# Fourier stage: the first group's folds moved into the last RG-LRU head, DFT tables from buffers of their own, last sums in other PSUM banks

## The chip, the cores and the metric

The kernel runs on one core of one Trainium2 chip. A core has five engines with instruction queues of their own: TensorE (PE in the profile), VectorE (DVE), ScalarE (ACT), GpSimd (POOL) and SyncE (SP); SP is used here only to issue DMA transfers. The metric is the time of one execution on the device in microseconds (us), as the median of several runs.

## The reference, cut to what matters

The reference is a trunk of two layers over 1024 latent tokens with a prefix of 256 context tokens, width 1024. The first layer projects its normed input with one matrix and splits the result in two halves with a SiLU gate each: an RG-LRU (eight heads of 128 channels, a recurrence run in both directions) and a Fourier mixer (four groups of 256 channels); both halves, gated, go through one output projection. The second layer is a retention layer, which this change leaves alone. The Fourier mixer is a 2D DFT over tokens and channels of each group, of which the real part is kept, and then one small matrix for each group:

```python
def fourier_branch(z, w_f):
    B_, T, W = z.shape
    zg = z.astype(jnp.float32).reshape(B_, T, FNET_GROUPS, FNET_GROUP_DIM)
    f = jnp.real(jnp.fft.fft2(zg, axes=(1, 3), norm='ortho'))
    y = jnp.einsum('btgi,gij->btgj', f, w_f.astype(jnp.float32))
    return y.reshape(B_, T, W).astype(z.dtype)

def even_mixer(h, hc, w_in, w_out, ...):
    ...
    ya, yca = rglru_branch(xa, xca, conv_w, conv_b, wa, ba, wx, bx, lam)
    yb = fourier_branch(xb, w_f)
    y = jnp.concatenate([ya * jax.nn.silu(ga), yb * jax.nn.silu(gb)], axis=-1) @ w_out
```

## The kernel before, in words

**Split operands.** Every product that must keep float32 accuracy is made from two parts: `split` casts an operand to fp32r (the high part, on ScalarE, or on VectorE with `he="v"`) and subtracts to get the low part (on VectorE, or on GpSimd with `le="g"`). `acc3` then issues three matmuls: high by high, high by low, low by high. A weight tile therefore passes through a DMA, a cast and a subtraction before TensorE can use it.

**The RG-LRU heads** (the loop over `n`, lines 437 to 482). Each head projects its input, makes gates, and ends in three scans on VectorE, an addition and a product with the gate `sga`, whose result goes to `ya_d` in DRAM. While head 7 runs, the projection of the first two channel tiles of the Fourier stage is already made (`four_z(8)` and `four_z(9)`).

**The Fourier groups** (the loop over `g`, lines 544 to 678). For each of the two channel tiles of a group, the tokens are *folded*: the first half of the sequence plus and minus the mirrored second half (`ze`, and `zc` for the context), with two single columns scaled apart (`zsp`). The folds of the two tiles are combined (`zss`, and `ze` and `zc` in place) and split (`zxh`, `zxl`, `zh`, `zl`). TensorE multiplies them with the combined channel matrix (`pa`, `pac`, `pn`), ScalarE and VectorE split the sums (`ah`, `al`), and the second set of products (`pd`, function `dftmm`, and `pcx` for the context) uses the DFT tables `dh` and `dl`. The result `y` is put together on VectorE, multiplied with the gate `sgb` (line 677) and written to `yb_d` by a DMA on SP's queue (line 678). Each group has two such halves, `ct` 0 and 1. The tables are made once, in group 0, by `dft_tables`: four raw pieces `dr` are loaded into the buffers of the ring `wr`, which the projection weights use too, cast on VectorE, and subtracted on GpSimd.

**PSUM.** Tiles with the tag `aux` share four banks, tiles with the tag `mm` four others. `pa`, `pn`, `pd`, `pcx` and the columns of the modulation vectors (`mod_a`, `mod_c`) are `aux`; the projections `pj` and `po` are `mm`.

**The output projection** begins when the Fourier stage ends. Its weights come through `w1tile`: a load into `wr` (printed as `wr<-in_wout`) by SP, a cast on ScalarE, a low part on VectorE or GpSimd in turn. Their buffers lie in pools that are allocated after the Fourier pools `four_in`, `four_out` and `fconst` are released, so in memory that these held.

**What sets the order.** The program is written for a scheduler that orders the instructions of each engine from dependencies and priorities; `tc.high_priority(offset=...)` moves what is written under it ahead by that offset. Each engine, and SP's DMA queue, then works strictly in that order: an instruction that waits holds back all that stand behind it in its queue. A pool's place in memory comes from the order in which pools are allocated, and a tile that lies over released memory waits for the last users of what lay there. `mod_next` makes one column block of the modulation vectors: `mod_a` on TensorE from a loaded `modw`, a copy `modr` on VectorE, and in a later call `mod_c` on TensorE, which VectorE reads for `sh` and `gs`.

Of the kernel before, what the change touches and what calls it, by code (L numbers as in the profile page):

```python
# [8 lines left out]
F32 = mybir.dt.float32  # L9
# [7 lines left out]
P = 128  # L17
# [8 lines left out]

OW0, OW1, OWE, OWF = [120, 140, 120, 150]
# [28 lines left out]
def _build(ctx, nc, tc, I, out, dbg):  # L56
# [306 lines left out]
    fz = pool("four_z")  # L363
    def channel_mats(g):
        cd = wp.tile([P, 2, 2, P], F32, tag="wr", name="cd", bufs=WRB)
        nc.sync.dma_start(cd, I["cd"])
        fw = fz.tile([P, 2, 256], F32, tag="fw", name="fw")
        nc.sync.dma_start(fw, I["fw"][g])
        pc = ps.tile([P, 2, 256], F32, tag="aux", name="cwp", bufs=4)
        for m in range(2):  # L370
            for k in range(2):
                mm(pc[:, m, :], cd[:, k, m, :], fw[:, k, :], k == 0, k == 1)
        f_ = fz.tile([P, 2, 256], F32, tag="cwf", name="cwf")
        h_ = fz.tile([P, 2, 256], F32R, tag="cwh", name="cwh")
        l_ = fz.tile([P, 2, 256], F32R, tag="cwl", name="cwl")
        nc.scalar.copy(f_, pc)
        split(f_, h_, l_)
        return f_, h_, l_
# [59 lines left out]
    for n in range(8):  # L438
# [4 lines left out]
        if n < 7:  # L443
            xa, gw = lru_in(n + 1)
        else:
            cw0 = channel_mats(0)
            zf0 = four_z(8)
# [24 lines left out]
        nga = gate_a(n + 1) if n < 7 else four_z(9)  # L472
# [10 lines left out]
    zs0 = [zf0, nga]  # L483
# [32 lines left out]

    fc = pool("fconst")
    cts = fc.tile([P, 260], F32, name="cts")
    nc.scalar.dma_start(cts, I["dftx"])
    dh = fc.tile([P, 2, 1028], F32R, name="dh")  # L520
    dl = fc.tile([P, 2, 1028], F32R, name="dl")
    COSE, COSO, SINE, SINO = (0, 258), (258, 256), (514, 256), (770, 258)
    fp = pool("four_out")
    fq = pool("four_in")
# [10 lines left out]
    def dft_tables():  # L535
        for j in range(2):
            for b in range(2):
                s = slice(b * 514, (b + 1) * 514)
                dr = wp.tile([P, 514], F32, tag="wr", name="dr", bufs=WRB)
                nc.sync.dma_start(dr, I["dftc"][:, j, s])  # L540
                split(dr, dh[:, j, s], dl[:, j, s], he="v", le="g")

    for g in range(4):
# [3 lines left out]
        zz = []  # L547
        for ct in range(2):
            z = zs0[ct]
            if g:  # L550
                z = four_z(8 + 2 * g + ct)
                mod_next()
            s2 = fq.tile([P, 2], F32, tag=f"zsp{ct}", name="zsp", bufs=1)
            nc.vector.tensor_scalar(out=s2[:, 0:1], in0=z[:, 512:513], scalar1=1.0 / 32, scalar2=None, op0=ALU.mult)
            nc.vector.tensor_scalar(out=s2[:, 1:2], in0=z[:, T + 129:T + 130], scalar1=1.0 / 16, scalar2=None, op0=ALU.mult)
            t = [s2]
            for e, op in ((0, ALU.add), (1, ALU.subtract)):
                w = fq.tile([P, 512], F32, tag=f"ze{e}{ct}", name=f"ze{e}", bufs=1)
                wc = fq.tile([P, P], F32, tag=f"zc{e}{ct}", name=f"zc{e}", bufs=1)
                (nc.vector if ct else nc.gpsimd).tensor_tensor(out=w.rearrange("p (two n) -> p n two", two=2),  # L560
                                        in0=z[:, 0:512].rearrange("p (n two) -> p n two", two=2),
                                        in1=z[:, T:512:-1].rearrange("p (n two) -> p n two", two=2), op=op)
                nc.vector.tensor_tensor(out=wc, in0=z[:, T + 1:T + 129], in1=z[:, NT + 1:T + 129:-1], op=op)
                t += [w, wc]
            zz.append(t)
        zx = [fq.tile([1, 512], F32R, tag=f"zx{p}", name=f"zx{p}") for p in "hl"]
        split(zz[0][1][0:1, :], *zx)
        zcx, zsx = zz[0][2][0:1, :], zz[0][0][0:1, :]
        for i, (a, b) in enumerate(zip(*zz)):
            if i == 0:  # L570
                zs = fq.tile([P, 2], F32, tag="zss", name="zss")
                nc.vector.tensor_tensor(out=zs, in0=a, in1=b, op=ALU.add)
            else:
                nc.vector.tensor_tensor(out=b, in0=a, in1=b, op=ALU.add if i < 3 else ALU.subtract)
                if i > 2:
                    nc.gpsimd.memset(b[0:1, :], 0.0)
        zf = []
        for e in range(2):
            zh = fq.tile([P, 512], F32R, tag=f"zh{e}", name=f"zh{e}")
            zl = fq.tile([P, 512], F32R, tag=f"zl{e}", name=f"zl{e}")  # L580
            split(zz[1][1 + 2 * e], zh, zl)
            zf.append((zz[1][2 + 2 * e], zh, zl))
        sgb = [gate_b(2 * g), None]
        if not g:
            dft_tables()
# [34 lines left out]
        for ct in range(2):  # L620
# [13 lines left out]
            def dftmm(e, par, blk):  # L634
                next(side, None)
                o = ps.tile([P, 512], F32, tag="aux", name="pd", bufs=4)
                b0, bn = blk
                ah, al = A[e, par]
                for j in range(2):
                    acc3(o[:, :bn], ah[:, j, cs], al[:, j, cs], dh[:, j, b0:b0 + bn], dl[:, j, b0:b0 + bn], j == 0, j == 1)  # L640
# [42 lines left out]
    fq.release()  # L683
    fp.release()
    fc.release()
    fz.release()
# [733 lines left out]
```

## Time and profile before

| | before |
|---|---|
| median of 3 runs | 1973.33 us |
| lowest and highest run | 1972.36 and 1985.31 us |
| the profiled run's own time | 1979.08 us |
| span of its trace | 1977.3 us |
| TensorE busy, share of the span | 95% |
| VectorE, ScalarE, GpSimd busy | 68%, 44%, 31% |
| mean granted TensorE clock | 0.97 |

The rows of the profile come from one execution, the profiled run; its time is 5.75 us above the median. TensorE is the busiest engine. Times in the timelines are in us from the start of the span. What an engine waited for stands in brackets in a timeline, as the idle time ahead of an instruction and the instruction that ended it.

### The profile page before, as it was taken

How to read it: one execution, taken by the hardware profiler on the slowest of the kernel's cores; microseconds unless marked ns; L12 is line 12 of the kernel's file. 1: busy time of each engine (PE TensorE's matmuls, PEld its weight loads, DVE VectorE, ACT ScalarE, POOL GpSimd, SP SyncE). 2: the span in 40 equal slices, each digit the busy share in tenths (PEclk: the TensorE clock that was granted, in tenths of full speed). 3: DMA queues.
4: the chain of work that ended last, by engine and by line, in shares of the span. 5: the costliest groups of instructions: out<-in, count | busy, mean ns of one | idle time of the engine just before them, and what ended most of it. 6: DMA issues, size and time to landing. Idle time of an engine off the chain costs nothing. (4 is left out here: it accounts for less than half of the span.)

```text
span 1977.3 us, 27858 instructions
## 1 busy us (share of the span) xinstructions
PE 1878.3 (95%) x10418; PEld 1592.5 (81%) x10418; DVE 1342.3 (68%) x1952; ACT 877.7 (44%) x1459; POOL 621.5 (31%) x407
## 2 busy tenths in 40 slices
PE   7999999899999999998988999999999799999997
PEld 3788888788888788887877889898898577877886
DVE  6787788742334515687798877778776685767766
ACT  5576667522222433364632433424334455554552
POOL 2411211302112241243455242252430133444444
PEclk8999999979999899999999999999999899999998
DMA  7221222322212362345834746547457656565544
GB/s 281 90 78 62 96 67 89 107 82 97 90 58 72 129 210 94 127 154 156 275 95 146 244 127 213 183 146 256 125 179 255 221 194 194 179 200 175 184 126 155
DMA packets 167559, 297.18 MB, mean 150 GB/s; under 512 B 15200, under 2 KB 94464, under 8 KB 166272
## 3 DMA queue, kind: packets, MB, share of 16 engines
q1 hardware_dynamic: 135824, 273.20, 42.5%
q10 hardware_dynamic: 31504, 22.16, 3.5%
q8 instruction: 82, 1.34, 0.3%
q14 instruction: 53, 0.43, 0.1%
q0 software_dynamic: 96, 0.04, 0.0%
HBM read 212.51 MB, written 82.84 MB: 149 GB/s over the span
## 5 line engine op out<-in xcount | busy, mean ns | idle before, releaser
L63 POOL TENSOR_TENSOR wl<-wr,wh 128x512 fp32r<-128x512 f32 (+1 forms) x80 | 149.4, 1870 | 376.3 <-ACT wh L69 365.9
L69 ACT CAST w<-wr 128x1024 fp32r<-128x1024 f32 x140 | 146.7, 1049 | 195.9 <-PE pst L58 115.7
L65 DVE TENSOR_TENSOR w<-wr,w 128x1024 fp32r<-128x1024 f32 x112 | 145.1, 1295 | 112.1 <-ACT w L69 112.1
L58 PE MATMUL pj<-xh,wl 128*128 128x512 f32 x512 | 203.0, 396 | 3.3 <-POOL wl L63 3.3
L58 PE MATMUL pj<-xh,wh 128*128 128x512 f32 x512 | 204.6, 401 | 1.0 <-ACT wh L69 0.6
L58 PE MATMUL pj<-xl,wh 128*128 128x512 f32 x512 | 202.7, 396 | 1.2 <-POOL xl L63 1.1
L58 PE MATMUL pst<-xh,w 128*128 128x512 f32 x512 | 164.8, 396 | 6.4 <-DVE w L65 6.4
L58 PE MATMUL po<-xh,w 128*128 128x512 f32 x512 | 163.9, 393 | 0.0
L63 POOL TENSOR_TENSOR w<-wr,w 128x1024 fp32r<-128x1024 f32 x28 | 70.8, 2530 | 165.6 <-ACT w L69 164.0
L58 PEld LDWEIGHTS pst<-xh,w 128*128 128x128 f32 x512 | 97.3, 190 | 27.0 <-DVE w L65 6.9
L58 PEld LDWEIGHTS pj<-xh,wl 128*128 128x128 f32 x512 | 97.0, 189 | 24.5 <-POOL wl L63 4.1
L58 PEld LDWEIGHTS pj<-xh,wh 128*128 128x128 f32 x512 | 96.7, 189 | 23.3 <-issue 1.4
L58 PEld LDWEIGHTS pj<-xl,wh 128*128 128x128 f32 x512 | 96.8, 189 | 22.1 <-POOL xl L63 2.1
L58 PEld LDWEIGHTS po<-xh,w 128*128 128x128 f32 x512 | 96.2, 188 | 19.7 <-issue 0.5
L69 ACT CAST st<-st 128x256 fp32r<-128x256 f32 (+2 forms) x128 | 53.6, 433 | 124.0 <-DVE st L969 56.2
L69 ACT CAST wh<-wr 128x512 fp32r<-128x512 f32 (+1 forms) x80 | 63.3, 793 | 92.3 <-DMA wr<-in_win 33.4
L58 PE MATMUL pds<-vp,kh 128*128 128x512 f32 x288 | 93.6, 407 | 8.7 <-ACT kh L1118 8.4
L58 PE MATMUL pst<-xl,w 128*128 128x512 f32 x256 | 100.6, 393 | 0.0
L58 PE MATMUL po<-stp,qt 128*128 128x512 f32 x384 | 97.8, 401 | 2.8 <-DVE stp L65 2.4
L58 PE MATMUL po<-xl,w 128*128 128x512 f32 x256 | 99.9, 390 | 0.0
L58 PE MATMUL pst<-w,xh 128*128 128x256 f32 x512 | 93.0, 284 | 0.7 <-DVE w L65 0.7
L58 PE MATMUL pj<-xc,wh 128*128 128x256 f32 x512 | 91.2, 278 | 0.0
(313 smaller groups left out, 4863.6 us busy)
## 6 DMA issues: line engine op xcount, KB each, us to landing
wr<-in_w SPq DMA_DIRECT2D x72, 512.0 KB, 4.5
vp<-v_d SPq DMA_DIRECT2D x44, 512.0 KB, 4.9
qt<-qs_d SPq DMA_DIRECT2D x32, 640.0 KB, 4.0
wr<-in_win SPq DMA_DIRECT2D x32, 512.0 KB, 3.6
modw<-in_modw SPq DMA_DIRECT2D x32, 512.0 KB, 3.6
wr<-in_wout SPq DMA_DIRECT2D x32, 512.0 KB, 3.6
qs_d<-st SPq DMA_DIRECT2D x64, 256.0 KB, 2.6
wr<-in_wout SPq DMA_DIRECT2D x56, 256.0 KB, 2.7
```

What stands on the lines that cost most here:

```text
L58: nc.tensor.matmul(o, lhsT=a, rhs=b, start=start, stop=stop)
L63: nc.gpsimd.tensor_tensor(out=o, in0=x, in1=hh, op=ALU.subtract)
L65: nc.vector.tensor_tensor(out=o, in0=x, in1=hh, op=ALU.subtract)
L69: nc.scalar.copy(h, x)
```

## The change

Four things are changed. First, the folds of group 0 become a function `fold` with a pool of its own, and are called in the last RG-LRU head; the combination and the splits of a group become `channel_folds`, which for group 0 runs at a raised priority (`OF0 = 40`). Second, the DFT tables have raw buffers of their own (two, in the pool `fconst`), are eight separate tiles, their high parts are cast on ScalarE, and `dft_tables` is called ahead of the group loop. Third, the sums `pd` of the last half of the last group take PSUM tiles with the tag `mm`. Fourth, the pool `four_in` is allocated ahead of `fconst` and released after it.

```diff
+    fo = pool("four_fold")
+
+    def fold(z, ct):
+
+        s2 = fo.tile([P, 2], F32, tag=f"zsp{ct}", name="zsp", bufs=1)
...
+        return t
...
-            zf0 = four_z(8)
+            zz0 = [fold(four_z(8), 0)]
...
-        nga = gate_a(n + 1) if n < 7 else four_z(9)
+        if n < 7:
+            nga = gate_a(n + 1)
+        else:
+            zz0.append(fold(four_z(9), 1))
...
+    fq = pool("four_in")
+
+    def channel_folds(zz, off):
+
+        with tc.high_priority(offset=off):
+            zx = [fq.tile([1, 512], F32R, tag=f"zx{p}", name=f"zx{p}") for p in "hl"]
+            split(zz[0][1][0:1, :], *zx)
+            zs = fq.tile([P, 2], F32, tag="zss", name="zss")
...
+                split(zz[1][1 + 2 * e], zh, zl)
+                zf.append((zz[1][2 + 2 * e], zh, zl))
+        return zx, zz[0][0][0:1, :], zz[0][2][0:1, :], zs, zf
+
     fc = pool("fconst")
     cts = fc.tile([P, 260], F32, name="cts")
     nc.scalar.dma_start(cts, I["dftx"])
-    dh = fc.tile([P, 2, 1028], F32R, name="dh")
-    dl = fc.tile([P, 2, 1028], F32R, name="dl")
-    COSE, COSO, SINE, SINO = (0, 258), (258, 256), (514, 256), (770, 258)
+    dr = [fc.tile([P, 514], F32, tag="dr", name="dr", bufs=2) for _ in range(4)]
+
+    dh = [[fc.tile([P, 514], F32R, name=f"dh{j}{b}") for b in range(2)] for j in range(2)]
+    dl = [[fc.tile([P, 514], F32R, name=f"dl{j}{b}") for b in range(2)] for j in range(2)]
+    COSE, COSO, SINE, SINO = (0, 0, 258), (0, 258, 256), (1, 0, 256), (1, 256, 258)
     fp = pool("four_out")
-    fq = pool("four_in")
...
-                dr = wp.tile([P, 514], F32, tag="wr", name="dr", bufs=WRB)
-                nc.sync.dma_start(dr, I["dftc"][:, j, s])
-                split(dr, dh[:, j, s], dl[:, j, s], he="v", le="g")
-
+        for b in range(2):
+            for j in range(2):
+                raw = dr[2 * b + j]
+                nc.sync.dma_start(raw, I["dftc"][:, j, b * 514:(b + 1) * 514])
+                split(raw, dh[j][b], dl[j][b], le="g")
+
+    dft_tables()
     for g in range(4):
...
-                o = ps.tile([P, 512], F32, tag="aux", name="pd", bufs=4)
-                b0, bn = blk
+                o = ps.tile([P, 512], F32, tag="mm" if g == 3 and ct else "aux", name="pd", bufs=4)
+                i, b0, bn = blk
...
-    fq.release()
     fp.release()
     fc.release()
+    fq.release()
+    fo.release()
     fz.release()
```

Apart from line and tile numbers, the instructions of each engine stand in the same order as before except at two places: where the first Fourier group begins, and where the last one ends.

The first place, on TensorE, before: `mod_c` and `mod_a` belong to the modulation vectors, `pj` is the projection for the gate of the group's second half, `pa` the first channel product.

```order
1554 L58 MATMUL mod_c<-sel,modr 128x2
1555 L162 MATMUL mod_a<-modw,s_83 32x128 x16
1556 L58 MATMUL pj<-xh_104,wh 128x512
1557 L58 MATMUL pj<-xl_105,wh 128x512
1558 L58 MATMUL pj<-xh_104,wl 128x512
1559 L58 MATMUL pa<-cwh,zh_3231 128x256
1560 L58 MATMUL pa<-cwl,zh_3231 128x256
```

On TensorE, after:

```order
1554 L59 MATMUL mod_c<-sel,modr 128x2
1555 L163 MATMUL mod_a<-modw,s_83 32x128 x5
1556 L59 MATMUL mod_c<-sel,modr 128x2
1557 L163 MATMUL mod_a<-modw,s_83 32x128 x11
1558 L59 MATMUL pa<-cwh,zh_3256 128x256
1559 L59 MATMUL pa<-cwl,zh_3256 128x256
1560 L59 MATMUL pa<-cwh,zl_3257 128x256
```

The second `mod_c`, which stood behind the first `pa` products before, stands inside `mod_a` now, and the `pj` matmuls stand behind the first products of `pa`.

The same place on VectorE, before: `b` and `t` are the last RG-LRU head's, `sga` is its gated result, then come the folds.

```order
289 L471 TENSOR_TENSOR b_2979<-b_2979,t_2981 128x1280
290 L471 TENSOR_TENSOR b_2980<-b_2980,t_2982 128x1280
291 L474 SCALAR_TENSOR_TENSOR t_2981<-r_2977,b_2979 128x1280
292 L475 SCALAR_TENSOR_TENSOR t_2982<-r_2978,b_2980 128x256
293 L71 CAST dh<-dr 128x514
294 L477 SCALAR_TENSOR_TENSOR t_2982<-r_2978,t_2982,b_2980 128x1024
295 L479 TENSOR_TENSOR t_2981<-t_2981,t_2982 128x1280
296 L480 TENSOR_TENSOR sga<-t_2981,sga 128x1280
297 L554 TENSOR_SCALAR zsp<-z 128x1
298 L555 TENSOR_SCALAR zsp<-z 128x1
299 L563 TENSOR_TENSOR zc_3201<-z 128x128
300 L563 TENSOR_TENSOR zc_3205<-z 128x128
```

On VectorE, after, from the folds of the second channel tile to the reading of `mod_c`:

```order
302 L376 TENSOR_TENSOR ze_3197<-z 128x256x2
303 L66 TENSOR_TENSOR zl_3257<-ze_3193,zh_3256 128x512
304 L550 TENSOR_TENSOR ze_3197<-ze_2987,ze_3197 128x512
305 L379 TENSOR_TENSOR zc_3198<-z 128x128
306 L496 SCALAR_TENSOR_TENSOR t_2995<-r_2991,b_2993 128x1280
307 L550 TENSOR_TENSOR zc_3198<-zc_2988,zc_3198 128x128
308 L66 TENSOR_TENSOR zl_3261<-ze_3197,zh_3260 128x512
309 L497 SCALAR_TENSOR_TENSOR t_2996<-r_2992,b_2994 128x256
310 L499 SCALAR_TENSOR_TENSOR t_2996<-r_2992,t_2996,b_2994 128x1024
311 L501 TENSOR_TENSOR t_2995<-t_2995,t_2996 128x1280
312 L502 TENSOR_TENSOR sga<-t_2995,sga 128x1280
313 L185 TENSOR_SCALAR sh<-mod_c,modb 128x2
```

The folds, the combination and the splits now stand ahead of the scans and among them, and `sh`, which reads `mod_c` and frees it for the next one, comes right behind `sga`. Before, it stood between the last two splits `zl` of the folds. The second `mod_c` writes the PSUM tile that `sh` reads, and waits for `sh`.

The same place on SP's DMA queue, before:

```order
77 L481 DMA ya_d<-sga 128x1280
78 L540 DMA dr<-in_dftc 128x514 x4
79 L172 DMA modw<-in_modw 128x1024 x2
80 L238 DMA wr<-in_win 128x1024
81 L481 DMA ya_d<-sga 128x1280
82 L172 DMA modw<-in_modw 128x1024 x2
83 L366 DMA cd<-in_cd 128x512
84 L678 DMA yb_d<-y 128x1280
```

On SP's DMA queue, after:

```order
77 L503 DMA ya_d<-sga 128x1280
78 L173 DMA modw<-in_modw 128x1024 x2
79 L239 DMA wr<-in_win 128x1024
80 L173 DMA modw<-in_modw 128x1024
81 L503 DMA ya_d<-sga 128x1280
82 L173 DMA modw<-in_modw 128x1024
83 L385 DMA cd<-in_cd 128x512
84 L584 DMA dr<-in_dftc 128x514 x4
```

The four raw pieces of the DFT tables (`dr`) were loaded between the two writes of `ya_d`, and are now loaded behind the last of them, behind `modw` and `cd`.

The second place, on SP's DMA queue, before: `wr<-in_wout` loads the weights of the output projection, `yb_d<-y` writes the results of the last group's two halves, the `st` are operands of the next stage and constants.

```order
126 L701 DMA wr_5854<-in_wout 128x1024
127 L701 DMA wr_5924<-in_wout 128x1024
128 L720 DMA st<-in_mskE 128x512
129 L722 DMA lg<-in_lg 128x8
130 L724 DMA kx<-in_kx 128x6
131 L726 DMA st<-in_qx 128x256
132 L678 DMA yb_d<-y 128x1280
133 L701 DMA wr_6134<-in_wout 128x1024
134 L701 DMA wr_6192<-in_wout 128x1024
135 L678 DMA yb_d<-y 128x1280
136 L505 DMA st<-ya_d 128x512 x2
```

On SP's DMA queue, after:

```order
127 L736 DMA st<-in_mskE 128x512
128 L738 DMA lg<-in_lg 128x8
129 L740 DMA kx<-in_kx 128x6
130 L742 DMA st<-in_qx 128x256
131 L693 DMA yb_d<-y 128x1280
132 L526 DMA st<-ya_d 128x512
133 L693 DMA yb_d<-y 128x1280
134 L526 DMA st<-ya_d 128x512 x3
135 L717 DMA wr_5864<-in_wout 128x1024
136 L717 DMA wr_5934<-in_wout 128x1024
```

Four weight loads stood ahead of the last write of `yb_d` before, two of them ahead of the first; all stand behind both now, and behind three more loads of `st`.

## Rows read from the trace of the kernel before

**Rows 1.** The page of the profile: the span, and the busy time of TensorE (PE) as a share of it with its number of instructions.

```profile
span 1977.3 us, 27858 instructions
...
PE 1878.3 (95%) x10418; PEld 1592.5 (81%) x10418; DVE 1342.3 (68%) x1952; ACT 877.7 (44%) x1459; POOL 621.5 (31%) x407
```

**Rows 2.** The timeline of TensorE where the first Fourier group begins. Columns: start in us, busy us of the row, engine, line, operation with out<-in, tile shapes, count; in brackets the idle time in us ahead of the row and what ended it.

```profile
387.24 0.28 PE L58 MATMUL mod_c<-sel,modr 128*128 128x2 f32 x2
387.44 1.08 PE L162 MATMUL mod_a<-modw,s 128*32 128x128 f32 x32
389.12 0.50 PE L58 MATMUL pj<-xh,wh 128*128 128x512 f32 x1 [0.59 <-ACT wh L69]
...
392.18 0.50 PE L58 MATMUL pj<-xh,wl 128*128 128x512 f32 x1 [2.33 <-POOL wl L63]
395.89 0.58 PE L58 MATMUL pa<-cwh,zh 128*128 128x256 f32 x1 [3.21 <-ACT zh L69]
```

**Rows 3.** The same timeline further on: the first of the last sums (`pd`) of the first Fourier group.

```profile
413.06 0.42 PE L58 MATMUL pd<-dh,ah 128*128 128x258 f32 x1
```

**Rows 4.** Stretches of the span, one row each: from:to in us, length, then busy us and number of instructions of PE, PE weight loads, DVE, ACT and POOL, then the granted TensorE clock (1.00 is 2.4 GHz, 0.50 is 1.2 GHz), DMA share and GB/s.

```profile
395.90:416.90 21.00, 21.00 (x72) 17.33 (x73) 6.66 (x16) 4.34 (x9) 0.66 (x2) 0.50 0.05 21
...
659.70:666.10 6.40, 6.40 (x37) 4.65 (x36) 3.73 (x7) 2.94 (x7) 1.27 (x1) 1.00 0.82 247
666.10:673.00 6.90, 6.90 (x33) 6.69 (x32) 5.92 (x13) 4.00 (x9) 5.20 (x4) 0.51 0.71 231
...
679.70:683.20 3.50, 2.86 (x13) 2.89 (x14) 3.50 (x10) 2.45 (x5) 0.97 (x1) 0.51 0.08 34
1009.50:1016.00 6.50, 0.06 (x2) 0.05 (x1) 6.50 (x4) 1.77 (x4) 5.32 (x3) 0.87 0.24 69
1016.00:1021.10 5.10, 5.10 (x12) 4.08 (x13) 5.10 (x7) 2.00 (x3) 2.67 (x2) 0.50 0.05 18
```

**Rows 5.** The timeline of VectorE (DVE) from the end of the last RG-LRU head to the start of the first Fourier group.

```profile
370.61 2.22 DVE L71 CAST dh<-dr 128x514 fp32r<-128x514 f32 x3
372.74 4.89 DVE L471 TENSOR_TENSOR b<-b,t 128x1280 f32<-128x1280 f32 x2
377.56 2.81 DVE L474 TENSOR_TENSOR_SCAN t<-r,b 128x1280 f32<-128x1280 f32 x1
...
383.57 2.21 DVE L479 TENSOR_TENSOR t<-t,t 128x1280 f32<-128x1280 f32 x1
385.81 1.49 DVE L480 TENSOR_TENSOR sga<-t,sga 128x1280 f32<-128x1280 f32 x1
...
387.87 1.08 DVE L560 TENSOR_TENSOR ze<-z 128x512 f32<-128x512 f32 x1
388.78 0.29 DVE L563 TENSOR_TENSOR zc<-z 128x128 f32<-128x128 f32 x1
...
389.87 2.40 DVE L563 TENSOR_TENSOR zc<-z 128x128 f32<-128x128 f32 x1
...
396.71 0.67 DVE L65 TENSOR_TENSOR zl<-ze,zh 128x512 fp32r<-128x512 f32 x1
397.32 0.20 DVE L184 TENSOR_SCALAR sh<-mod_c,modb 128x2 f32<-128x2 f32 x1
```

**Rows 6.** The timeline of GpSimd (POOL) over the same stretch: three low parts of the DFT tables, and the low part of a projection weight.

```profile
371.16 5.12 POOL L63 TENSOR_TENSOR dl<-dr,dh 128x514 fp32r<-128x514 f32 x3 [16.35 <-DVE dh L71]
...
389.14 2.98 POOL L63 TENSOR_TENSOR wl<-wr,wh 128x1024 fp32r<-128x1024 f32 x1 [4.72 <-DVE zc L563]
```

**Rows 7.** The timeline of SyncE's DMA queue (SPq) over the same stretch; the time is that of issuing.

```profile
387.32 0.33 SPq L481 DMA_DIRECT2D ya_d<-sga  x1
...
393.05 0.38 SPq L366 DMA_DIRECT2D cd<-in_cd  x1
```

**Rows 8.** The view of the DMA issues, from 352 to 375 us: KB of each, and the median us from issue to landing.

```profile
dr<-in_dftc SPq DMA_DIRECT2D x4, 257.0 KB, 2.7
```

**Rows 9.** The timeline of TensorE at the end of the last Fourier group: a wait inside the last sums, the first matmul of the output projection, and its return after the last `pcx`.

```profile
680.34 0.55 PE L58 MATMUL pd<-dh,ah 128*128 128x256 f32 x1 [4.46 <-DVE y L667]
...
683.04 0.45 PE L58 MATMUL po<-xh,w 128*128 128x512 f32 x1
...
684.26 0.28 PE L58 MATMUL pd<-dh,ah 128*128 128x258 f32 x1
...
685.34 0.71 PE L58 MATMUL po<-xh,w 128*128 128x512 f32 x2
```

**Rows 10.** The timeline of SyncE's DMA queue over the same stretch.

```profile
668.61 6.31 SPq L701 DMA_DIRECT2D wr<-in_wout  x2
...
690.61 0.33 SPq L678 DMA_DIRECT2D yb_d<-y  x1
691.03 1.34 SPq L505 DMA_DIRECT2D st<-ya_d  x2
```

**Rows 11.** The timeline of VectorE over the same stretch: the low part of an output projection weight, and the last gated product of the Fourier stage.

```profile
682.03 1.22 DVE L65 TENSOR_TENSOR w<-wr,w 128x1024 fp32r<-128x1024 f32 x1
...
689.10 1.48 DVE L677 TENSOR_TENSOR y<-y,sgb 128x1280 f32<-128x1280 f32 x1
```

**Rows 12.** The timeline of ScalarE (ACT): the high part of an output projection weight.

```profile
679.90 1.04 ACT L69 CAST w<-wr 128x1024 fp32r<-128x1024 f32 x1
```

**Rows 13.** The view of the DMA issues, from 660 to 720 us, columns as in group 8.

```profile
wr<-in_wout SPq DMA_DIRECT2D x11, 512.0 KB, 4.4
```

More of the change, by code (lines that the diff above doesn't have):

```diff
@@ L25 @@
 NCH = T // P
+OF0 = 40
 OW0, OW1, OWE, OWF = [120, 140, 120, 150]
@@ L363, in _build @@
     fz = pool("four_z")
+    fo = pool("four_fold")
+    def fold(z, ct):
+        s2 = fo.tile([P, 2], F32, tag=f"zsp{ct}", name="zsp", bufs=1)
+        nc.vector.tensor_scalar(out=s2[:, 0:1], in0=z[:, 512:513], scalar1=1.0 / 32, scalar2=None, op0=ALU.mult)
+        nc.vector.tensor_scalar(out=s2[:, 1:2], in0=z[:, T + 129:T + 130], scalar1=1.0 / 16, scalar2=None, op0=ALU.mult)
+        t = [s2]
+        for e, op in ((0, ALU.add), (1, ALU.subtract)):
+            w = fo.tile([P, 512], F32, tag=f"ze{e}{ct}", name=f"ze{e}", bufs=1)
+            wc = fo.tile([P, P], F32, tag=f"zc{e}{ct}", name=f"zc{e}", bufs=1)
+            (nc.vector if ct else nc.gpsimd).tensor_tensor(out=w.rearrange("p (two n) -> p n two", two=2),
+                                    in0=z[:, 0:512].rearrange("p (n two) -> p n two", two=2),
+                                    in1=z[:, T:512:-1].rearrange("p (n two) -> p n two", two=2), op=op)
+            nc.vector.tensor_tensor(out=wc, in0=z[:, T + 1:T + 129], in1=z[:, NT + 1:T + 129:-1], op=op)
+            t += [w, wc]
+        return t
     def channel_mats(g):
@@ L482, in _build @@
         sga = nga
-    zs0 = [zf0, nga]
     if "ya" in dbg:
@@ L514, in load_y @@
             yield
+    fq = pool("four_in")
[4 more added lines that the diff above has]
+            zs = fq.tile([P, 2], F32, tag="zss", name="zss")
+            for i, (a, b) in enumerate(zip(*zz)):
+                if i == 0:
+                    nc.vector.tensor_tensor(out=zs, in0=a, in1=b, op=ALU.add)
+                else:
+                    nc.vector.tensor_tensor(out=b, in0=a, in1=b, op=ALU.add if i < 3 else ALU.subtract)
+                    if i > 2:
+                        nc.gpsimd.memset(b[0:1, :], 0.0)
+            zf = []
+            for e in range(2):
+                zh = fq.tile([P, 512], F32R, tag=f"zh{e}", name=f"zh{e}")
+                zl = fq.tile([P, 512], F32R, tag=f"zl{e}", name=f"zl{e}")
+                split(zz[1][1 + 2 * e], zh, zl)
+                zf.append((zz[1][2 + 2 * e], zh, zl))
+        return zx, zz[0][0][0:1, :], zz[0][2][0:1, :], zs, zf
     fc = pool("fconst")
@@ L535, in dft_tables @@
     def dft_tables():
-        for j in range(2):
-            for b in range(2):
-                s = slice(b * 514, (b + 1) * 514)
-                dr = wp.tile([P, 514], F32, tag="wr", name="dr", bufs=WRB)
-                nc.sync.dma_start(dr, I["dftc"][:, j, s])
-                split(dr, dh[:, j, s], dl[:, j, s], he="v", le="g")
+        for b in range(2):
[3 more added lines that the diff above has]
+                split(raw, dh[j][b], dl[j][b], le="g")
@@ L543, in _build @@
+    dft_tables()
     for g in range(4):
         cf, ch, cl = channel_mats(g) if g else cw0
[L547 to L550, printed above, removed]
+        zz = zz0
+        if g:
+            zz = []
+            for ct in range(2):
                 z = four_z(8 + 2 * g + ct)
                 mod_next()
[L553 to L582, printed above, removed]
+                zz.append(fold(z, ct))
+        zx, zsx, zcx, zs, zf = channel_folds(zz, 0 if g else OF0)
         sgb = [gate_b(2 * g), None]
-        if not g:
-            dft_tables()
         mod_next()
@@ L635, in dftmm @@
                 next(side, None)
-                o = ps.tile([P, 512], F32, tag="aux", name="pd", bufs=4)
-                b0, bn = blk
+                o = ps.tile([P, 512], F32, tag="mm" if g == 3 and ct else "aux", name="pd", bufs=4)
+                i, b0, bn = blk
                 ah, al = A[e, par]
                 for j in range(2):
-                    acc3(o[:, :bn], ah[:, j, cs], al[:, j, cs], dh[:, j, b0:b0 + bn], dl[:, j, b0:b0 + bn], j == 0, j == 1)
+                    acc3(o[:, :bn], ah[:, j, cs], al[:, j, cs], dh[j][i][:, b0:b0 + bn], dl[j][i][:, b0:b0 + bn], j == 0, j == 1)
                 return o
```

## The prediction

> **What bounds the kernel now.** The page comes first: TensorE is busy for 1878.3 of 1977.3 us [rows 1]. A part of the change is therefore worth only what it does to TensorE's idle time, or to the clock at which TensorE works. So I read TensorE's own timeline at the two places where the order of instructions changes, then the granted clock there, then the timelines of the engines that end TensorE's waits.
>
> At the first place, where Fourier group 0 begins, TensorE waits three times: 0.59 us for the cast of a projection weight, 2.33 us for its low part from GpSimd, 3.21 us for the cast of the first fold, 6.1 us in all [rows 2]. Then it is 100% busy for 21.0 us at a granted clock of 0.50, its lower level of 1.2 GHz [rows 4]. At the second place, the end of group 3, it waits 4.46 us inside the last sums for VectorE's last reading of an earlier sum (line 667) [rows 9], and works at 0.51 just after [rows 4]. Elsewhere no instruction changes its place, so I look for nothing there.
>
> **Place 1, the start of group 0.**
>
> *What goes.* Folds, combination and splits stand ahead of `sga` on VectorE now, so the wait of 3.21 us for the fold has nothing left to wait for. The `pj` behind the 0.59 and 2.33 us is moved behind `pa`, by when its weight is long there. Gain: 6.1 us.
>
> *What comes: the second `mod_c`.* It stands in the middle of `mod_a` and waits for `sh`, which stands behind `sga` in VectorE's queue. When is `sga` done? VectorE had three casts of tables at 370.61 [rows 5]; without them the two `b` products wait only for ScalarE's square root, until about 371.8, an estimate. They took 4.9 us beside GpSimd's low parts of the tables [rows 5, 6]; those are gone from here. A single two-input product of this size takes 1.49 us (row of `sga` [rows 5]), so two take about 2.9: 374.7. The folds follow. Their rows: two `ze` of 0.9 us each (from the start of one to that of the next operation), six or seven operations of about 0.6 us (`zl` is 0.67), `zc` at 0.29, in sum about 5.8, and 1.1 for the casts on ScalarE between them: 6.9 us, 381.6. The scans, the addition and `sga` ran from 377.56 to 387.22 or so (385.81 and 1.41 more) [rows 5]; less 0.3 us for a table cast and 0.7 us by which the addition (2.21) took longer than `sga` of the same size, 8.6 us: 390.2. The low part `wl` of a projection weight falls among this on GpSimd. What that costs is seen in one row: `zc`, 0.29 us alone, took 2.40 us while `wl` ran (389.14 to 392.12) [rows 5, 6]. I take these 2.1 us: `sga` ends at 392.3, `sh` (0.20) at 392.5. TensorE reaches the second `mod_c` at about 387.6 [rows 2], and idles 4.9 us.
>
> The Trainium skill (page "SBUF — State Buffer", the section on the shared port pair) makes this an exclusive lock: of a two-input VectorE operation and a GpSimd operation the second to start is held for the whole of the other. The row agrees: `zc` ended 0.15 us after `wl`. By the rule the loss could be the whole of `wl`, 2.98 us, and the sum below 0.9 us larger.
>
> *The tables.* Their loads stand behind the last `ya_d` and `cd` now, which went out at 387.32 and 393.05 [rows 7]; I put the first at about 392.5. Landing took 2.7 us in the middle [rows 8], and I take 4 among the neighbours: 396.5. A cast on ScalarE costs what a cast of this size costs there, about 0.6 us, beside idle time. GpSimd's low part took 1.7 us each [rows 6]; the third and fourth loads wait until a low part has freed one of two buffers. First two tables: 400.6; all four: about 406. The first `pd` came 17.2 us after the first `pa` [rows 2, 3]; from 392.5 that is 409 at half clock and some 5 us earlier if half of the way is at full clock. So the tables cost nothing, or little over a microsecond. I take 0.5 us.
>
> Idle time: 6.1 − 4.9 − 0.5 = **0.7 us** gained.
>
> *The clock.* Twenty-one busy us at 0.50 cost 10.5 us against full clock [rows 4]. The idle time ahead of them shrinks but stays, so a stretch at half clock stays too. How long? The nearest rows are 5.1 us after an idle gap at 1016.0, and 6.9 us at 666.1 to 673.0, where TensorE was 100% busy for 6.4 us before at full clock [rows 4]. From 6.9 to 21.0 I take the middle, 14: 7.0 us lost instead of 10.5, **3.5 us** gained. Bounds: nothing, and 8.0 us (5.1 instead of 21.0).
>
> Place 1 together: **4.2 us** gained; from −4.8 (the tables late, below) to 14.1 us (the whole 6.1 and 8.0).
>
> **Place 2, the end of group 3.**
>
> *What goes.* With `pd` in the `mm` banks, the last sums need no bank back from VectorE, so the 4.46 us go [rows 9]. The sums and the `pcx` that were left took 2.7 us at half clock and 1.1 at full clock [rows 9]; without the gap that is about 2.4 us from 675.9 on, so TensorE has done its last `pcx` at about 678 instead of 685.3.
>
> *What comes.* Nothing is left for TensorE but the output projection, and its weights are late. Before, the first two weight loads were issued from 668.61 on [rows 10], so the first `po` could start at 683.04 [rows 9]. Now they stand in SP's queue behind the last `yb_d`, which waits for VectorE's product `y` by `sgb`. That product lay at 689.10 to 690.6 [rows 11]. It stands behind ScalarE's Exps and VectorE's `msk` products, which are not moved much; ScalarE is spared two weight casts ahead of them, so I take it 0.5 us earlier: 690.1. Then on SP: `yb_d` (0.4), three loads `st` at about 0.5 each (two took 1.34 [rows 10]), and the first weight goes out at 692.0. It lands after 4.4 us [rows 13], 696.4. The cast takes 1.04 [rows 12]: 697.45. Two matmuls of `po` need the high part alone, the third waits for the low part of 1.22 us on VectorE [rows 11]. This takes some 0.35 us more, so it is as if `po` started at 697.8.
>
> Before, `po` returned for good at 685.34, having done 1.2 us of its work from 683.04 to 684.26 [rows 9], as if it started at 684.1. Difference: **13.7 us**. And TensorE restarts from 20 us of idleness: like the stretch from 1016.0, 5.1 busy us at 0.50, 2.6 us lost [rows 4]. Loss: **16.3 us**. Bounds: 13 (landing one us quicker, a shorter slow stretch) to 21 (the landing two us dearer, 10 busy us at half clock).
>
> What covers this? Nothing: the later steps of the output projection follow each other on a full TensorE, so the time isn't won back.
>
> **Sum.** −4.2 + 16.3 = +12.1 us. The profiled run took 1979.08 us, so 1991.2 against its own time; it lies 5.75 us above the median of 1973.33, so the forecast for the median is **1985.4 us**. About 1% (19.7 us, so 1953.6 to 1993.1) is what a measurement of this kernel can tell from no change.
>
> **The rivals.**
>
> *R: the clock comes back at once.* TensorE idles some 5 us at place 1 and then has work without end; if it is back at full clock after 5.1 busy us, as from 1016.0 [rows 4], place 1 gains 0.7 + 8.0 = 8.7 us, and the time is 1980.9. For it: a shorter gap ahead. Against it: the 6.9 us at half clock that began with no gap at all [rows 4]. The Trainium skill ("TensorE: Matmul & The Clock Gate", Part 1) says that the gate follows how busy TensorE has been of late, and opens fully once it works on without a break. By that rule R is what happens; the rows at 395.90 and 666.10, 100% busy at half clock, speak against it.
>
> *N: place 1 gains nothing.* `sga` is a few microseconds later still, or the stretch at half clock stays at 21 us: 1989.6.
>
> *S: slower by over 1%.* The place is the first `pd` of group 0, the price that of late tables. Beside VectorE's scans and the `pa` splits, GpSimd may need 3 us for each low part, like `wl` [rows 6], and the third load waits for the first of them. Then the fourth table is there at 411 and not at 406; TensorE idles 5 us in all and falls back to half clock for another 5.1 busy us: place 1 loses 0.7 − 4.5 − 2.5 + 1.5 (a little clock kept) = −4.8, and the time is 1994.4. It decides where low parts take over 2.5 us.
>
> *F: the weights are not late.* If the `yb_d` in front goes out soon, because VectorE gets to `y` by `sgb` with the sums ready 5 us earlier, the weights land during the last sums: 4.46 us and 1.4 us of clock (2.86 busy us at 0.51 [rows 4]) gained at place 2, 4.2 at place 1: 1963.3. Against it: the product stands behind the Exps.
>
> **How the numbers follow.** Forecast 0.52, R 0.17, N 0.13, S 0.10, F 0.08. The range from 1974 to 1995 holds the forecast with its bounds, R, N and most of S; F is left out. Faster by over 1% needs F and the best of place 1: 0.03. Slower by over 1%: S, and the dear ends of the forecast and N: 0.13. Within 1%: 0.84.
>
> **What would show it.** On TensorE near 387 the waits for `wl` and `zh` gone and one for VectorE's `sh` of 4 to 5 us in their place; a stretch at half clock after it of 7 to 21 us; a first `pd` that waits for GpSimd or not. Near 680 no wait for VectorE inside the last sums; one of some 20 us ahead of the first `po`, ended by ScalarE's cast of `w`; on SP the weight loads right behind `yb_d` and three `st`, at about 692. I am wrong if the last `yb_d` goes out before 685, if TensorE has other work in that gap, or if half clock at the start lasts as long as before.

## The result and the profile after

| | before | after |
|---|---|---|
| median (7 runs each) | 1975.43 us | 1993.06 us |
| lowest and highest | 1971.89 and 1985.31 us | 1984.1 and 1994.87 us |
| ratio | | 1.0073, 95% interval 1.0057 to 1.0089 |
| profiled run, its span | 1979.08, 1977.3 us | 1993.28, 1991.5 us |

The change makes the kernel slower by 0.73% (0.57% to 0.89%), about 14.4 us; the two profiled runs lie 14.2 us apart, the two medians 17.6 us. The forecast was 1985.4 us, 12.1 us more than the median of three runs that it started from (1973.33), in a range from 1974 to 1995.

The page of the profile after shows the same work and the same share of busy time on TensorE, give or take a percent; the answer isn't there [rows 1].

```profile
span 1991.5 us, 27845 instructions
...
PE 1880.6 (94%) x10418; PEld 1592.6 (80%) x10418; DVE 1341.3 (67%) x1948; ACT 880.0 (44%) x1463; POOL 621.5 (31%) x407
```

The first place, on TensorE's timeline. The waits for the weight's low part and for the fold [rows 2] are gone; one for VectorE's `sh` has come inside `mod_a`, and a short one for GpSimd's low part of a table inside the sums:

```profile
386.86 0.28 PE L59 MATMUL mod_c<-sel,modr 128*128 128x2 f32 x2
387.07 0.62 PE L163 MATMUL mod_a<-modw,s 128*32 128x128 f32 x10
390.93 0.38 PE L59 MATMUL mod_c<-sel,modr 128*128 128x2 f32 x2 [3.24 <-DVE sh L185]
391.24 0.86 PE L163 MATMUL mod_a<-modw,s 128*32 128x128 f32 x22
...
412.65 0.39 PE L59 MATMUL pd<-dl,ah 128*128 128x256 f32 x1 [0.50 <-POOL dl L64]
```

Why does `sh` come so late? On VectorE, the folds begin ahead of the scans, and `sh` is right behind `sga`:

```profile
371.07 2.89 DVE L490 TENSOR_TENSOR b<-b,t 128x1280 f32<-128x1280 f32 x2 [1.09 <-ACT t L489]
...
375.52 2.31 DVE L548 TENSOR_TENSOR zss<-zsp 128x2 f32<-128x2 f32 x1
...
381.11 2.81 DVE L496 TENSOR_TENSOR_SCAN t<-r,b 128x1280 f32<-128x1280 f32 x1
...
389.25 1.49 DVE L502 TENSOR_TENSOR sga<-t,sga 128x1280 f32<-128x1280 f32 x1
390.66 0.21 DVE L185 TENSOR_SCALAR sh<-mod_c,modb 128x2 f32<-128x2 f32 x1
```

`zss` adds two columns, an operation of about 0.1 us. It took 2.31 us because GpSimd made the low part of a projection weight at the time:

```profile
374.63 3.19 POOL L64 TENSOR_TENSOR wl<-wr,wh 128x1024 fp32r<-128x1024 f32 x1 [18.02 <-ACT wh L70]
```

It ended at 377.83 and the low part at 377.82; some 2.2 us were lost. In [rows 5, 6] the same met `zc`. The Trainium skill ("SBUF — State Buffer", section "Who interferes with whom") has the two engines exclude each other where a VectorE instruction with two inputs meets a GpSimd instruction that reads: the later one is blocked until the first has finished. The trace agrees: the two ends lie 0.01 us apart.

The clock, in stretches of the span (columns as in [rows 4]). TensorE is busy throughout in the first four and for 4.60 of 4.64 us in the last, at its lower level of 1.2 GHz:

```profile
392.45:406.05 13.60, 13.60 (x41) 9.84 (x40) 2.20 (x4) 5.92 (x10) 2.52 (x2) 0.50 0.48 156
484.60:498.20 13.60, 13.60 (x49) 11.13 (x48) 3.14 (x7) 4.09 (x8) 2.37 (x1) 0.50 0.13 42
570.00:573.30 3.30, 3.30 (x16) 3.10 (x15) 1.05 (x2) 1.56 (x4) 2.37 (x1) 0.50 0.00 0
658.70:672.30 13.60, 13.60 (x52) 11.64 (x53) 9.58 (x19) 5.24 (x12) 6.50 (x5) 0.50 0.53 173
...
698.36:703.00 4.64, 4.60 (x10) 3.20 (x11) 3.39 (x2) 3.14 (x3) 3.28 (x2) 0.50 0.63 241
```

The second place. On TensorE's timeline the wait inside the last sums [rows 9] is gone, and one of 21.39 us stands ahead of the output projection:

```profile
676.36 0.61 PE L59 MATMUL pcx<-cts,ac 128*128 128x130 f32 x4
698.36 0.80 PE L59 MATMUL po<-xh,w 128*128 128x512 f32 x1 [21.39 <-ACT w L70]
```

On SP's queue, the weight loads stand behind the last `yb_d` and three loads:

```profile
681.14 0.33 SPq L693 DMA_DIRECT2D yb_d<-y  x1
...
689.06 0.32 SPq L693 DMA_DIRECT2D yb_d<-y  x1
689.47 1.85 SPq L526 DMA_DIRECT2D st<-ya_d  x3
691.41 11.02 SPq L717 DMA_DIRECT2D wr<-in_wout  x6
```

The view of DMA issues from 691 to 700 us (KB each, median us to landing), and ScalarE's cast, which waits for the DMA:

```profile
wr<-in_wout SPq DMA_DIRECT2D x5, 512.0 KB, 6.5
```

```profile
697.26 1.04 ACT L70 CAST w<-wr 128x1024 fp32r<-128x1024 f32 x1 [1.98 <-DMA wr<-in_wout]
```

To see where the time went, the start of the same instruction in both traces is followed along the program. A change of the difference from one row to the next is what was lost or won between them:

| instruction | before | after | difference |
|---|---|---|---|
| ScalarE's third copy of `z`, last RG-LRU head | 351.89 | 351.18 | −0.71 |
| VectorE's `zss`, group 1 | 472.36 | 466.74 | −5.62 |
| `zss`, group 3 | 635.15 | 630.99 | −4.16 |
| ScalarE's last `ac`, group 3 | 668.61 | 666.54 | −2.07 |
| ScalarE's fifth copy of `po` into `acc` | 706.61 | 723.21 | +16.60 |
| a late `ha` of VectorE, second layer | 1971.90 | 1986.10 | +14.20 |

Place 1 won 4.9 us. Place 2 lost 18.7 us. The groups between lost 3.5 us, with instructions in the same order as before, at half clock: 13.6 us long in group 1 and in group 3, where there were 10.2 and 6.9 us before. What becomes of such a stretch is the last experiment. The 2.4 us that come back after place 2 lie in stages that the change doesn't touch. These are differences of two single executions; how far such a pair can be trusted is taken up with before_again and after_again.

### The profile page after: what moved, and what is told of

Same layout as the page of the kernel before. It is cut to its first block, busy times and chain, and to the rows that moved or that the text cites. A ratio compares the mean times of both kernels' runs of the same rounds, so it can differ in the third digit from the quotient of the medians.

```text
span 1991.5 us, 27845 instructions
## 1 busy us (share of the span) xinstructions
PE 1880.6 (94%) x10418; PEld 1592.6 (80%) x10418; DVE 1341.3 (67%) x1948; ACT 880.0 (44%) x1463; POOL 621.5 (31%) x407
```

## The experiments

The theory for place 2: the first buffers of the output projection's weights lie in memory that `y`, `spe`, `u` and others of the pool `four_out` held, so the scheduler puts their loads behind VectorE's last product and behind `yb_d`. The rival: the banks of the last sums. For place 1: `sh` behind `sga` is the wait that is left; the tables and the clock are open. "Gain at the start" is the change of the difference to the kernel before, from the copies of `z` to `zss` of group 1, as in the table above.

**old_banks.** One part undone:

```diff
-                o = ps.tile([P, 512], F32, tag="mm" if g == 3 and ct else "aux", name="pd", bufs=4)
+                o = ps.tile([P, 512], F32, tag="aux", name="pd", bufs=4)
```

> The changed kernel with one part undone: the last sums take the tag aux again, as before. Theory (the weights are late because their buffers lie over memory that VectorE's last product y holds, and so stand behind the last yb_d): the wait for VectorE inside the last sums comes back, 4 to 5 us, but inside time in which TensorE idles anyway; the first po starts within 1 us of the 698.4 of the changed kernel, and the time is within 3 us of it, so 14 to 20 us above the kernel before. Rival (the banks carry the loss): TensorE's wait ahead of the first po falls under 6 us, and the time comes to within 3 us of 1971, four below the kernel before.

Measured: 1.0076 (1.0053 to 1.0098), the same as the changed kernel. TensorE's timeline:

```profile
672.71 0.55 PE L59 MATMUL pd<-dh,ah 128*128 128x256 f32 x1 [2.29 <-DVE y L682]
...
693.28 0.80 PE L59 MATMUL po<-xh,w 128*128 128x512 f32 x1 [14.69 <-ACT w L70]
```

The wait inside the sums is back: 2.29 us here, and 2.24 us at 668.8. The wait ahead of the first `po` shrinks to 14.69 us, because the sums end later by these waits and by more work at half clock. `po` starts 5 us before the 698.4 that was expected, but the whole trace is 4.6 us ahead at the last `ac` by its shorter stretches at half clock. Lost at place 2: 18.8 us. The banks neither cause the loss nor change it.

**y_below.** Eight tiles go to a pool lower in memory:

```diff
+    fy = pool("four_y")
     fc = pool("fconst")
...
-            y = fp.tile([P, NT], F32, tag="y", name="y", bufs=1)
+            y = fy.tile([P, NT], F32, tag="y", name="y", bufs=1)
```

and so for `sgb`, `nb`, `spe`, `u`, `spc`, `sqe`, `v`.

> The changed kernel with eight tiles moved: sgb, nb, spe, u, spc, sqe, v and y come from a pool of their own that is allocated ahead of fconst, so lower in memory; nothing else. The output projection's first buffers then lie over the tables and the split sums, whose last user is TensorE's last pcx. Theory: the first weight load goes out right behind that pcx, at 677 to 678 instead of 691.4, lands in 4 to 5 us, and the first po starts at 683 to 684.5 instead of 698.4; of the 18.7 us lost at the end some 14 to 15 come back, so the time is within 4 us of the kernel before. Rival (ScalarE's Exps or the banks hold the start, and the place in memory does not matter): the first po stays behind 690, and the time at least 10 us above the kernel before.

Measured: 1.0000 (0.9980 to 1.0021). TensorE, SP's queue, ScalarE, and the view of DMA issues from 673 to 676 us:

```profile
680.57 0.79 PE L59 MATMUL po<-xh,w 128*128 128x512 f32 x1 [6.35 <-ACT w L70]
```

```profile
673.68 0.80 SPq L719 DMA_DIRECT2D wr<-in_wout  x2
678.74 0.33 SPq L694 DMA_DIRECT2D yb_d<-y  x1
...
688.03 0.33 SPq L694 DMA_DIRECT2D yb_d<-y  x1
```

```profile
676.63 1.28 ACT L756 ACT_TABLE_LOAD   x1
...
679.48 1.04 ACT L70 CAST w<-wr 128x1024 fp32r<-128x1024 f32 x1
```

```profile
wr<-in_wout SPq DMA_DIRECT2D x2, 512.0 KB, 3.9
```

The first weight goes out with the last `pcx` (673.61), ahead of both `yb_d`. It lands in 3.9 us, not in 6.5. What is late next is ScalarE: the cast stands behind the table load and a few Exps and begins 1.9 us after the landing. The wait is 6.35 instead of 21.39 us, the loss at place 2 2.0 instead of 18.7 us. The place of these eight tiles in memory is the cause of the loss: nothing else was changed here.

**banks_only.** The kernel before with the tag `mm` alone.

> The kernel before with one part of the change alone: the last sums take the tag mm. Theory: the 4.46 us inside the last sums go, the weights are loaded as early as before, and what is late next is ScalarE's cast of the first weight, at about 681; the first po for good starts about 3 us earlier in effect, so the time is 1 to 6 us below the kernel before. Rival (the banks carry the loss of the changed kernel): 5 us or more above the kernel before.

Measured: 0.9993 (0.9980 to 1.0007), no change that can be told. TensorE's timeline:

```profile
678.77 0.79 PE L58 MATMUL po<-xh,w 128*128 128x512 f32 x1 [3.39 <-ACT sqe L655]
...
680.81 1.22 PE L58 MATMUL po<-xh,w 128*128 128x512 f32 x2 [0.82 <-DVE w L65]
```

The 4.46 us went and 3.39 + 0.82 us came ahead of the output projection. The weight was as early as expected, its cast done at 678.44; but the first `po` started only at 678.77, behind ScalarE's `sqe`, which copies one of the last sums (ended 678.72). The sums stand in the `mm` banks now, which `po` uses too, so the wait for a bank seems to have moved there; no run separates this. The second wait is for the weight's low part. The change of banks alone is worth nothing: at place 2 this kernel even loses 1.3 us on the kernel before. The idle time is about the same, and 6.8 us at half clock lie there, where the kernel before had 3.5 [rows 4].

**sh_early.** The `mod_c` of group 0 at a raised priority:

```diff
         sgb = [gate_b(2 * g), None]
+        with tc.high_priority(offset=0 if g else 60):
+            mod_flush()
         mod_next()
```

> The changed kernel with one step moved: the mod_c that is due when the first Fourier group begins, and its readers sh and gs, are made at a priority raised by 60, so that sh stands ahead of the last scan parts and of sga on VectorE. Theory: the 3.24 us that TensorE waited for sh are gone, pa starts about 3 us earlier, and the time is 2 to 5 us below the changed kernel (12 to 15 us above the kernel before). Rival (the loads of the DFT tables, which stand behind ya_d and cd on SP's queue, decide): the first pd waits for a table in place of it, and less than 1 us is gained. What the clock does is open: if an idle gap starts the stretch at half clock, it is under 7 us now; if not, it stays near 13.7 us.

Measured: 1.0058 (1.0037 to 1.0080). A miss in its purpose:

```profile
385.03 0.58 PE L59 MATMUL mod_c<-sel,modr 128*128 128x2 f32 x2 [3.12 <-DVE sh L185]
```

`mod_c` moved ahead by 6 us on TensorE, but `sh` only ahead of the last scan on VectorE, at 384.8. The wait moved and did not go. Expected were 2 to 5 us below the changed kernel; the gain over it is within the intervals.

**y_below_sh.** Both, with the priority raised by 200.

> The kernel y_below with one more step moved: the mod_c that is due at the start of group 0 and its readers sh and gs get a priority raised by 200, so that on VectorE sh stands ahead of the folds, and on TensorE mod_c stands well ahead of mod_a. (With 60 the wait only moved: sh stood behind the first scan, and TensorE waited 3.12 us for it at 381.9 instead of 3.24 at 387.7.) Theory: no wait for sh is left, pa starts at about 388, and from the projections before to the folds of group 1 the kernel gains 2.5 to 3.5 us on y_below; the time is 1 to 5 us below the kernel before. Rival (the DFT tables, loaded behind the last ya_d, come too late for pd now): a wait of 2 us or more ahead of a pd, and a gain under 1 us.

Measured: 0.9968 (0.9955 to 0.9980): 6 us faster than the kernel before, and faster than the changed kernel. TensorE's timeline at the start of group 0:

```profile
385.84 1.08 PE L163 MATMUL mod_a<-modw,s 128*32 128x128 f32 x32
...
404.25 0.38 PE L59 MATMUL pd<-dl,ah 128*128 128x256 f32 x1 [0.55 <-POOL dl L64]
```

No wait for `sh` is left. The tables are late by 0.55 us in one place, so the rival falls. The gain at the start is 11.0 us against 3.1 in y_below. Of the difference 2.8 us are waits (3.36 us for `sh` in y_below, 0.55 us here); the rest goes with the clock: 6.8 us at half clock here, 20.5 in y_below. One profile of each can't say how much of that belongs to the step, since the same start had 13.6 us in the changed kernel. The runs say that the clock is better as a whole: the mean granted clock of the nine runs is 0.973 (0.970 to 0.975), that of the 15 runs of the kernel before on the same chip 0.9705 (0.968 to 0.973). At place 2 this kernel loses 3.8 us on the kernel before, y_below 2.0. The stretches at the start (columns as in [rows 4]), with TensorE busy throughout:

```profile
384.00:390.80 6.80, 6.80 (x71) 5.53 (x70) 6.02 (x6) 0.97 (x2) 0.00 (x0) 1.00 0.23 81
390.90:397.60 6.70, 6.70 (x23) 4.99 (x22) 1.38 (x2) 3.06 (x6) 0.91 (x1) 0.50 0.68 230
```

**y_below_tables.** y_below with the raw tables through the ring `wr` and cast on VectorE again:

```diff
-                raw = dr[2 * b + j]
+                raw = wp.tile([P, 514], F32, tag="wr", name="dr", bufs=WRB)
...
-                split(raw, dh[j][b], dl[j][b], le="g")
+                split(raw, dh[j][b], dl[j][b], he="v", le="g")
```

and the call of `dft_tables` in its old place.

> The kernel y_below with the second part of the change undone: the raw DFT tables come through the ring wr again and are cast on VectorE, as before; folds, banks and pools stay. Theory (the tables' part is worth something only by leaving the ring to the projection weights): the weight of the gate's second half is cast 5 us or more later, so TensorE waits for it behind pa; from the projections before to the folds of group 1 this kernel is 1 to 4 us behind y_below. Rival (the early folds carry all of the gain at the start): within 0.7 us of y_below there.

Measured: 1.0068 (1.0047 to 1.0089). At the start it loses 5.2 us on the kernel before, 8.3 us more than y_below. TensorE, and SP's queue:

```profile
389.32 0.38 PE L59 MATMUL mod_c<-sel,modr 128*128 128x2 f32 x2 [1.69 <-DVE sh L185]
400.75 1.08 PE L163 MATMUL mod_a<-modw,s 128*32 128x128 f32 x16 [11.05 <-DMA modw<-in_modw]
```

```profile
356.73 3.57 SPq L583 DMA_DIRECT2D dr<-in_dftc  x3
389.16 0.33 SPq L503 DMA_DIRECT2D ya_d<-sga  x1
395.70 0.33 SPq L583 DMA_DIRECT2D dr<-in_dftc  x1
397.11 1.55 SPq L173 DMA_DIRECT2D modw<-in_modw  x2
```

The theory was right in the ring and wrong in who waits and how long. The casts of the tables stand behind `sh` on VectorE (the first at 389.94, the next, which waits for the write of `ya_d`, at 394.12), so a buffer of the ring comes free late; the fourth table load goes out at 395.70 only, and `modw`, which stands behind it on SP's queue, keeps TensorE waiting for 11.05 us. GpSimd's first low part of a table began at 394.12 too. With the tables as before, the early folds make the start slower, so the second part of the change is one that they need. Whether the ring, the casts on VectorE or the place of the tables in memory (one of the casts waits for `ya_d`) weighs most is not separated: this kernel has all three.

**folds_high.** The pool `four_in` on top again as before, and the first weight buffers in a pool that lies over it alone:

```diff
-    fq = pool("four_in")
...
     fp = pool("four_out")
+    fq = pool("four_in")
...
-    wa, wb = [pool(f"w1{i}", side="right") for i in "ab"]
+    wa, wc, wb = [pool(f"w1{i}", side="right") for i in "acb"]
```

> The changed kernel with the pool order of before (four_in on top again, behind four_out) and the first buffers of the output projection's weights split into two pools, so that the first pool lies over the splits of the folds alone. The weights are loaded ahead of mskE again; but four_in now lies over memory of the RG-LRU's pools, and the combination of the folds stands behind sga again. Theory (the place in memory decides at both ends): the first po starts 1 to 3 us after the last pcx, so the loss at the end is gone; but at the start pa waits for zl, behind a wait for sh, 4 to 6 us together, and the gain there falls from 4.9 us to under 3. Time 1 to 6 us below the kernel before. Rival (the early folds of the single tiles alone carry the start): the gain at the start stays above 4 us.

Measured: 1.0038 (1.0020 to 1.0057), slower where faster was expected. TensorE at the start, and then at the end:

```profile
393.49 0.59 PE L59 MATMUL mod_c<-sel,modr 128*128 128x2 f32 x2 [5.65 <-DVE sh L185]
```

```profile
681.10 0.80 PE L59 MATMUL po<-xh,w 128*128 128x512 f32 x1 [4.05 <-ACT sqe L669]
...
683.14 1.22 PE L59 MATMUL po<-xh,w 128*128 128x512 f32 x2 [0.81 <-DVE w L66]
...
696.47 0.80 PE L59 MATMUL po<-xh,w 128*128 128x512 f32 x1 [2.35 <-ACT w L70]
...
699.01 1.22 PE L59 MATMUL po<-xh,w 128*128 128x512 f32 x2 [1.32 <-POOL w L64]
```

The start came as expected: 5.65 us of waiting, a gain of 2.1 us. That gain is against the first profile of the kernel before; against the second it is a loss of 0.7 us. At the end the first `po` started 4.05 us after the last `pcx`, not 1 to 3, again behind `sqe`. And the second weight's split parts lie in the second pool, over `y`; it was cast at 694.42 only, and TensorE waited 2.35 and 1.32 us for it, partly in a stretch at half clock. Lost there: 7.3 us. The expectation looked at the first weight only.

**before_again** and **after_again**: both kernels unchanged, one more profile each.

> The kernel before, unchanged, profiled a second time: how much of the clock at the start of group 0 belongs to the program? If the stretch at half clock is set by the idle gaps ahead of it, it is near 23.9 us again (within 3.4). If it differs from run to run, it may be 10 us shorter, as in banks_only, whose instructions at that place are those of the kernel before (13.7 us); then the gain of 3.5 us that the forecast put on the clock is no property of the change. The idle times (0.6, 2.3 and 2.9 to 3.2 us) stay in either case.

> The changed kernel, unchanged, profiled a second time. If the clock follows the gaps, its stretch at half clock behind the wait for sh is 13.7 us again (within 3.4), and those of groups 1 and 3 are 13.7 us again; if it differs from run to run, these three differ by 7 us or more. TensorE's wait ahead of the first po is 20 to 22 us in either case, and what is lost between the last pac of group 3 and the second output tile is 16 to 19 us against the kernel before.

Stretches at half clock in the second profile of the changed kernel:

```profile
392.45:406.05 13.60, 13.60 (x41) 9.93 (x42) 2.50 (x4) 5.91 (x10) 2.53 (x2) 0.50 0.50 165
488.05:491.40 3.35, 3.35 (x16) 3.15 (x15) 1.25 (x2) 1.70 (x4) 2.37 (x1) 0.50 0.00 0
563.15:576.70 13.55, 13.55 (x50) 11.28 (x49) 3.54 (x8) 4.09 (x8) 2.37 (x1) 0.50 0.12 39
662.15:668.90 6.75, 6.75 (x30) 6.53 (x30) 5.73 (x11) 4.00 (x9) 5.21 (x4) 0.50 0.69 238
```

In the second profile of the kernel before, the one at the start of group 0:

```profile
393.10:410.10 17.00, 14.62 (x47) 11.35 (x48) 7.29 (x13) 4.68 (x9) 1.99 (x7) 0.50 0.19 74
```

The same program gets other stretches: in groups 1, 2 and 3 of the changed kernel 13.6, 3.3 and 13.6 us became 3.35, 13.55 and 6.75 us. At the start of group 0 the kernel before had 23.9 us and then 17.0, and banks_only, with the same instructions there, 13.7 us in two pieces; the changed kernel had 13.6 us twice. The two second profiles were taken on one chip, which need not be that of the first two. Idle times repeat within 0.3 us, the wait ahead of `po` was 21.56 us, and place 2 lost 17.7 us against the first profile of before and 18.5 against the second. Between the two second profiles, whose copies of `z` in the last head start at the same time, place 1 gains 2.07 us (`zss` of group 1 starts at 469.12 and 467.05). From those copies to `zss` the kernel before took 120.5 and 117.6 us, banks_only 115.7, the changed kernel 115.6 twice: depending on the profile of the same old start, place 1 gains from 4.9 us to 0.1.

## Why the prediction was right

**Place 2**, the term that decides, was right in mechanism and order, and 2.4 us too small (16.3 forecast, 18.7 measured). TensorE was done at 676.97 (forecast 678), the last `yb_d` went out at 689.06 (690.1), the weight at 691.41 (692.0), `po` started at 698.36 (697.45). Two terms make the difference. The first weight took 5.85 us from the issue to the cast, where the forecast took 4.4 from a row whose loads mostly went out in pairs [rows 13]. Six of them stand in a row now, right behind three loads of `st`; five show 6.5 us, against 3.9 for two in y_below, which had no other load just ahead. And the forecast set `yb_d` by the clock time of the trace before, though all that leads to it had moved ahead by 2.07 us; measured against that pace, the product came about 1 us later than forecast.

**The banks** cost and gave nothing, as the forecast had it: the 4.46 us were inside time in which TensorE waits for the weights anyway. old_banks shows it for the changed kernel. In banks_only, where the weights are early, the gain was lost to a wait behind `sqe`, which the forecast had not seen.

**Place 1** was 4.9 us, forecast 4.2, but not by its terms. The idle time gained 6.1 − 3.2 − 0.5 (a wait for a table at 412) = 2.4 us, where 0.7 was forecast: `sga` was done at 390.7 and not at 392.3. The 2.1 us for GpSimd's low part came, on `zss`; but the `b` products were done at 373.9 and not at 374.7, and VectorE never waited for ScalarE's casts, for which the forecast had put 1.1 us. The tables cost the 0.5 us that were forecast, by luck: the fourth was to be ready at 406 and was at 412.6, since ScalarE's last two casts for them came at 408.09 and 410.62 only, in their places behind `ah` and `spe`; TensorE reached the sum that needs it no earlier than 412.15. The clock's 3.5 us were not a property of the change: two profiles of the kernel before differ by 6.9 us in the length of that stretch, which is about 3 us of time. What repeats is the idle time, 2.1 to 2.4 us less in both pairs of profiles; that place 1 as a whole came out near its forecast is luck.

**What was put at nothing.** The groups between the places lost 3.5 us and the stages after them won 2.4 us, both at unchanged instructions. The forecast had neither. That they nearly cancel is luck too; without them the two places make +13.8 us.

**The rivals.** S and F did not come: the wait for a table was 0.5 us and each low part took 1.3 us, not over 2.5, and the weights were late. N, that place 1 gains nothing, can't be ruled out: against banks_only it gains 0.1 us. R did not come: after 3.24 us of idleness TensorE worked without a break, 1.5 us at 1.00 and then 13.6 us at 0.50. The Trainium skill ("TensorE: Matmul & The Clock Gate", Part 1) has the gate open while TensorE works on; by that it should not have fallen in y_below_sh at 390.8. There TensorE had been busy for 60.77 of 60.80 us at 1.00 (330.0 to 390.8). The measurement decides: here the clock fell without a gap.

**The cause** of the loss is that the last tiles of the Fourier stage came to lie under the first weight buffers of the next one; y_below, which moves these tiles alone, shows it. What put them there follows from the order of the pools: the fourth part has `four_in` low in memory, which lets the folds run while the RG-LRU's pools are still held, and puts `four_out` on top. y_below keeps the first and undoes the second. How much the memory of the new buffers (`four_fold`, `dr`) adds was not run apart, and folds_high, which undoes the pool order, changes the weight pools as well.

## What to carry to other kernels

When a pool is moved, look at what will lie over it in the next stage: a tile that covers the last-used tiles of the stage before is loaded last, and an in-order DMA queue then holds all later loads behind that. Give long-lived results and early-freed operands pools of their own, and put those that end last where no first load of the next stage will land. Before a gain is credited to the clock, profile the unchanged kernel twice.

## What was not expected of the hardware

The stretches at half clock differ between executions of the same program, by 7 to 10 us in place and length (13.6 and 3.35 us in group 1), with TensorE 100% busy and idle times equal to within 0.3 us. In groups 1 to 3 of the two profiles of the changed kernel the fall lies inside the products `pa` each time (484.5, 569.9, 658.6; 488.0, 563.1, 662.1). What starts such a stretch no run here shows. Busy 6.8 us at half clock are 3.4 us of time, so these stretches are likely to make part of the spread of the runs: of the seven runs of the changed kernel, the fastest (1984.1 us) had a mean granted clock of 0.970, the other six 0.964 to 0.967 at 1990.73 to 1994.87 us.
